# Output projection of a decoder layer: the low weights' pass of 320 token columns against two of 160

## The chip, the cores and the metric

The kernel runs on one core of one Trainium2 chip. The metric is the device time of one execution in microseconds (us). For the kernel before it is 1702.18 us, the median of 3 runs (1701.84 to 1702.85).

## The reference, cut to what matters

The program is one step of a decoder layer on 320 tokens: 256 of a prompt and 8 x 8 of samples, 2048 features wide, all in float32.

```python
xn = rms_norm(x, g_mix)
z = xn @ w_in                      # split into B, C, h, q, k, v, gate_c, gate_a
y_conv = (b_gate * conv_out) @ w_conv_out
y_attn = attn @ w_attn_out
merged = jax.nn.sigmoid(gate_c) * y_conv + jax.nn.sigmoid(gate_a) * y_attn
h = x + merged @ w_o               # the output projection: 2048 x 2048
hn = rms_norm(h, g_ffn)
h = h + (jax.nn.silu(hn @ w_gate) * (hn @ w_up)) @ w_down
```

The change lies in `merged @ w_o`.

## The kernel before, in words

Activations lie transposed: features on the 128 partitions, the `T` = 320 tokens along the free axis, one slice of 128 features per k. A product is computed as weights (128 x 128, loaded into TensorE as the stationary operand) times 320 token columns, summed over k in a PSUM tile.

To keep float32's precision with the type fp32r, every weight and every activation is split into a high part (rounded to fp32r) and a low part (the rest). A product of the two then takes three passes: high weights x high activations, high weights x low activations, low weights x high activations. Low x low is left out.

All large products go through one helper, `product` (L116 to L143). It takes two column blocks of 128 output features (`c` = 0 and 1), each with a PSUM tile `ps[c]` of its own. Weights come in tiles of four k and both column blocks (128 x 4 x 256). `load_cols` (L96) issues the transfer from SyncE's queue into `wraw` (4 buffers), ScalarE rounds it into `whi` (L93), VectorE subtracts to give `wlo` (L94; 3 buffers each). For every k and c of the tile, L133 to L137 then issue the three passes into `ps[c]`, in the order (whi, xh), (whi, xl), (wlo, xh). In the last tile of a product, all k of c = 0 come ahead of those of c = 1. A pass is one instruction of the program and two rows of the profile: the weight load (engine PEld) and the matmul (PE). Each pass loads its weights anew, also where the one before it had the same.

The order of the kernel: the k and v columns of `w_in` (a helper of their own, L284), q, then C, H, B with the convolution (L725 to L769), during which attention is interleaved as side work, then gates and the two branch outputs (L810 to L833), the output projection (L842 to L861), and the feed-forward network in two halves (L868 on).

The output projection runs over eight pairs of column blocks (`mp`) with 16 k each. Its activations are `m_h` and `m_l`, its product has the name `wo`. After each pair of blocks VectorE adds the product to the residual `hT` (L850), ScalarE and VectorE make the next high and low parts (`hh_t`, `hl_t`, L851 and L852), and GpSimd sums squares into `hacc` (L857 to L861), which the feed-forward part reads at L881, after its first gate product (`fg`). The attention's side work is not active any more in this stage.

Two other places are used as price rows below. The prompt scores (`prompt_scores`, L434) multiply queries and keys in fp32r with 256 columns (L442) and 128 columns (L447), each pass with a load of 128 weight columns. The transposes of the attention weights (`prompt_pt`, L495) move 128 columns with a load of 128 columns.

```python
for mp in range(8):                                            # L842
    c0 = mp * CW
    ps = product(
        lambda k0, n: load_cols(w_o, k0, n, c0), KC,
        lambda k: m_h[:, k, :], lambda k: m_l[:, k, :], "wo",
    )
```

Of the kernel before, what the change touches and what calls it, by code (L numbers as in the profile page):

```python
# [17 lines left out]
T = TP + NB * TS  # L18
# [8 lines left out]
P = 128  # L27
# [13 lines left out]
def hybrid_layer(ctx: ExitStack, tc: tile.TileContext, a: dict, o: list):  # L41
# [17 lines left out]
    def ps_acc(name):  # L59
        return acc.tile([P, 512], F32, tag="acc", name=name)  # L60
# [6 lines left out]
    def u(s):  # L67
        uid[0] += 1
        return f"{s}_{uid[0]}"

    def after(*marks):

        es = ExitStack()
        for m in marks:
            es.enter_context(tc.issue_after(m.ins))
        return es
# [3 lines left out]
    def tmp(tag, name):  # L80
        return wk.tile([P, UL], F32, tag=tag, name=u(name))
# [14 lines left out]
    def load_cols(w, k0, n, c0, behind=()):  # L96
        raw = raw_tile()
        nc.sync.dma_start(
            raw[:, :n, :],
            w[k0 * P:(k0 + n) * P, c0:c0 + CW].rearrange("(k p) n -> p k n", p=P),  # L100
        )
        hi, lo = part_tiles()
        with after(*behind):
            split_to(hi[:, :n, :], lo[:, :n, :], raw[:, :n, :])
        return hi, lo
# [5 lines left out]
    def tick():  # L111
        if side_work[0] is not None:
            with after(*last.values()):
                next(side_work[0], None)

    def product(load, nk, xh, xl, name, tiles=None, loaded=None, before=None, late=None):  # L116

        ps = [ps_acc(u(name)) for _ in range(2)]
        k0 = 0
        for n in tiles or [min(KT, nk - k) for k in range(0, nk, KT)]:  # L120
            hi, lo = load(k0, n)
            if loaded:
                loaded()
            order = [(k, c) for k in range(n) for c in range(2)]
            if k0 + n == nk:
                order.sort(key=lambda kc: kc[1])
            for k, c in order:
                kc = k0 + k
                if before and c == 0:
                    before(kc)  # L130
                if late and k0 + n == nk and (k, c) == (2, 1):
                    late(ps)
                for i, (w, x) in enumerate(((hi, xh), (hi, xl), (lo, xh))):  # L133
                    last["mm"] = nc.tensor.matmul(  # L134
                        ps[c][:, :T], w[:, k, c * P:(c + 1) * P], x(kc),
                        start=(kc == 0 and i == 0), stop=(kc == nk - 1 and i == 2),
                    )  # L137
            k0 += n
            while pending:
                with after(last["lo"]):  # L140
                    pending.pop(0)()
            tick()
        return ps  # L143
# [61 lines left out]
    def in_pair(c0, name, **kw):  # L205
        return product(lambda k0, n: load_cols(w_in, k0, n, c0), KC, xh, xl, name, **kw)
# [476 lines left out]
    def load_q(j, gp):  # L683
        def load(k0, n):
            raw = raw_tile()
            for two in range(2):
                c0 = O_Q + j * 512 + two * 256 + gp * P
                mark["q"] = nc.sync.dma_start(
                    raw[:, :n, two * P:(two + 1) * P],
                    w_in[k0 * P:(k0 + n) * P, c0:c0 + P].rearrange("(k p) n -> p k n", p=P),  # L690
                )
            hi, lo = part_tiles()
            for g in range(2):
                src = raw[:, :n, :].rearrange("p k (two g d) -> p k two g d", two=2, g=2)[:, :, :, g]
                dst = [
                    w[:, :n, g * P:(g + 1) * P].rearrange("p k (two d) -> p k two d", two=2) for w in (hi, lo)
                ]
                split_to(dst[0], dst[1], src)
            return hi, lo
        return load  # L700
# [17 lines left out]
    for j in range(2):  # L718
        for gp in range(2):
            ps = product(load_q(j, gp), KC, xh, xl, "q")  # L720
            pending.append(lambda j=j, gp=gp, ps=ps: q_out(j, gp, ps))
# [3 lines left out]
    for cp in range(4):  # L725
        c_sb = []
        ps = in_pair(O_C + cp * CW, "C")
# [4 lines left out]
        ps = in_pair(O_H + cp * CW, "H")  # L732
# [26 lines left out]
        ps = in_pair(O_B + cp * CW, "B")  # L759
# [18 lines left out]
    m_h = mm.tile([P, KC, T], F32R, name="m_h")  # L778
    m_l = mm.tile([P, KC, T], F32R, name="m_l")
# [15 lines left out]
    def load_ao(c0):  # L795
        def load(k0, n):
            j = k0 // KT
            raw = raw_tile()
            for par in range(2):
                r0 = (2 * j + par) * GRP * HD  # L800
                nc.sync.dma_start(
                    raw[par * 64:(par + 1) * 64, :, :],
                    w_ao[r0:r0 + GRP * HD, c0:c0 + CW].rearrange("(g d) n -> d g n", d=HD),
                )
            hi, lo = part_tiles()
            split_to(hi, lo, raw)
            return hi, lo
        return load

    for mp in range(8):  # L810
        c0 = mp * CW
        sg = {}
        for nm, off, tag in (("gc", O_GC, "ta"), ("ga", O_GA, "tb")):
            ps = in_pair(off + c0, nm)
            for c in range(2):
                t = tmp(tag, nm)[:, :T]
                nc.vector.tensor_mul(t, ps[c][:, :T], rb)
                nc.scalar.activation(t, t, AF.Sigmoid)
                sg[nm, c] = t
        ps = product(  # L820
            lambda k0, n: load_cols(w_co, k0, n, c0), 8,
            lambda k: cv_h[:, k, :], lambda k: cv_l[:, k, :], "yc",
        )
        for c in range(2):
            nc.vector.tensor_mul(sg["gc", c], ps[c][:, :T], sg["gc", c])
        ps = product(
            load_ao(c0), 8, lambda k: at_h[:, k, :], lambda k: at_l[:, k, :], "ya",
        )
        for c in range(2):
            t = sg["ga", c]  # L830
            nc.vector.tensor_mul(t, ps[c][:, :T], t)
            nc.vector.tensor_add(t, t, sg["gc", c])
            split_to(m_h[:, mp * 2 + c, :], m_l[:, mp * 2 + c, :], t)  # L833
# [8 lines left out]
    for mp in range(8):  # L842
        c0 = mp * CW
        ps = product(
            lambda k0, n: load_cols(w_o, k0, n, c0), KC,
            lambda k: m_h[:, k, :], lambda k: m_l[:, k, :], "wo",
        )
        for c in range(2):
            k = mp * 2 + c
            nc.vector.tensor_add(hT[:, k, :], ps[c][:, :T], hT[:, k, :])  # L850
            nc.scalar.activation(hh_t[:, k, :], hT[:, k, :], AF.Copy, scale=g_ffn[:, k:k + 1])  # L851
            nc.vector.scalar_tensor_tensor(  # L852
                hl_t[:, k, :], hT[:, k, :], g_ffn[:, k:k + 1], hh_t[:, k, :].bitcast(F32),
                op0=ALU.mult, op1=ALU.subtract,
            )
            if k == 0:
                nc.gpsimd.tensor_tensor(hacc, hT[:, k, :], hT[:, k, :], op=ALU.mult)  # L857
            else:
                t = tmp("tc", "sq")[:, :T]
                nc.gpsimd.tensor_tensor(t, hT[:, k, :], hT[:, k, :], op=ALU.mult)  # L860
                nc.gpsimd.tensor_tensor(hacc, hacc, t, op=ALU.add)  # L861
# [6 lines left out]
    for half in range(2):  # L868
# [67 lines left out]
# [3 lines that stand above are left out]
                lambda k0, n: load_cols(w_d, f0 + k0, n, c0), nf,  # L939
                lambda k: a_h[:, k, :], lambda k: a_l[:, k, :], "dn",  # L940
                late=next_last if half == 1 and mp == 7 else None,
            )
            if half == 1 and mp == 7:
                break
            for c in range(2):
                k = mp * 2 + c
                nc.vector.tensor_add(hT[:, k, :], hT[:, k, :], ps[c][:, :T])
            if half == 1:
                pc = [ps_aux(u("fa")) for _ in range(2)]
                for c in range(2):  # L950
                    k = mp * 2 + c
                    for t, (t0, tn) in enumerate(TOK):
                        nc.tensor.transpose(pc[c][:tn, t * P:(t + 1) * P], hT[:, k, t0:t0 + tn], ident)
                for c in range(2):
                    k = mp * 2 + c
# [7 lines left out]
    k = KC - 1  # L963
# [109 lines left out]
```

## Time and profile before

| | |
|---|---|
| median of 3 runs | 1702.18 us |
| the profiled execution | 1702.27 us |
| its span, first to last instruction | 1700.5 us |
| granted TensorE clock, mean | 0.997 |
| passes named `wo` | 768, of 128x320 |
| start of the first and the last of them | 638.8 and 751.3 us |
| length recorded for one: matmul, weight load | 310 ns, 188 ns |
| VectorE, ScalarE, GpSimd busy in 638.9 to 751.6 us | 62.0, 42.2, 29.0 us |
| DMA engines busy in that stretch | 47% |

The profile is of one execution. Its first part gives each engine's busy time, its fourth the chain of work that ended last, followed backwards from the last instruction. The chain can also be read in order of time, and the instructions of a stretch can be listed one by one (the timeline). Recorded lengths of matmuls and loads include latency, so rows of successive passes overlap; the distance between two starts tells what a pass costs in a stream. A load is listed by the tiles of the pass that it is for.

### The profile page before, as it was taken

How to read it: one execution, taken by the hardware profiler on the slowest of the kernel's cores; microseconds unless marked ns; L12 is line 12 of the kernel's file. 1: busy time of each engine (PE TensorE's matmuls, PEld its weight loads, DVE VectorE, ACT ScalarE, POOL GpSimd, SP SyncE). 2: the span in 40 equal slices, each digit the busy share in tenths (PEclk: the TensorE clock that was granted, in tenths of full speed). 3: DMA queues.
4: the chain of work that ended last, by engine and by line, in shares of the span. 5: the costliest groups of instructions: out<-in, count | busy, mean ns of one | idle time of the engine just before them, and what ended most of it. 6: DMA issues, size and time to landing. Idle time of an engine off the chain costs nothing.

```text
span 1700.5 us, 27713 instructions
## 1 busy us (share of the span) xinstructions
PE 1682.2 (99%) x11600; PEld 1670.9 (98%) x11600; DVE 863.3 (51%) x1231; ACT 643.5 (38%) x945; POOL 81.3 (5%) x127
## 2 busy tenths in 40 slices
PE   8999999999999999999999999999999999999996
PEld 7999999999999999999999999999999999999996
DVE  7667554444444445556454545433345545454443
ACT  6445443333333333334333333322233333333432
POOL 1001221000000001220000000000000000000000
PEclk9999999999999999999999999999999999999998
DMA  7754554555555544444444444444444444445442
GB/s 217 216 153 142 161 151 131 147 150 151 151 152 151 149 149 149 149 149 149 149 149 150 149 150 152 152 152 150 149 150 149 149 149 149 149 151 171 149 140 96
DMA packets 256719, 258.22 MB, mean 152 GB/s; under 512 B 9091, under 2 KB 251615, under 8 KB 256433
## 3 DMA queue, kind: packets, MB, share of 16 engines
q1 hardware_dynamic: 254128, 249.86, 47.8%
q0 software_dynamic: 2128, 5.92, 1.2%
q8 instruction: 91, 1.49, 0.4%
q10 hardware_dynamic: 336, 0.66, 0.2%
q14 instruction: 36, 0.29, 0.1%
HBM read 253.29 MB, written 5.08 MB: 152 GB/s over the span
## 4 chain that ended last, share of the span: by engine, by line
PE 95%; issue 2%; DMA 1%; DVE 1%; SPq 0%; POOL 0%; ACT 0%; DVEq 0%; POOLq 0%; ACTq 0%
PE fg L134 18%; PE fu L134 18%; PE dn L134 18%; PE wo L134 7%; PE ga L134 7%; PE gc L134 7%; PE C L134 3%; PE B L134 3%; PE H L134 3%; PE ya L134 3%; PE yc L134 3%; PE q L134 2%; DMA wraw<-in_w_in_dram 0%; DMA rel<-in_rel_bias_dram 0%; PE po L508 0%
## 5 line engine op out<-in xcount | busy, mean ns | idle before, releaser
L94 DVE TENSOR_TENSOR wlo<-wraw,whi 128x1024 fp32r<-128x1024 f32 (+1 forms) x481 | 573.8, 1195 | 703.9 <-ACT whi L93 701.3
L93 ACT ACTIVATE whi<-wraw 128x1024 fp32r<-128x1024 f32 (+1 forms) x481 | 493.3, 1030 | 852.4 <-PE dn L134 198.2
L134 PE MATMUL dn<-a_h,whi 128*128 128x320 f32 x704 | 218.5, 310 | 0.0
L134 PE MATMUL fu<-hh_t,whi 128*128 128x320 f32 x704 | 217.4, 309 | 0.0
L134 PE MATMUL dn<-a_h,wlo 128*128 128x320 f32 x704 | 217.3, 309 | 0.0
L134 PE MATMUL dn<-a_l,whi 128*128 128x320 f32 x704 | 217.2, 309 | 0.0
L134 PE MATMUL fg<-hh_t,whi 128*128 128x320 f32 x704 | 217.2, 309 | 0.0
L134 PE MATMUL fg<-hl_t,whi 128*128 128x320 f32 x704 | 217.2, 309 | 0.0
L134 PE MATMUL fg<-hh_t,wlo 128*128 128x320 f32 x704 | 217.2, 309 | 0.0
L134 PE MATMUL fu<-hl_t,whi 128*128 128x320 f32 x704 | 217.2, 308 | 0.0
L134 PE MATMUL fu<-hh_t,wlo 128*128 128x320 f32 x704 | 217.2, 308 | 0.0
L134 PEld LDWEIGHTS fu<-hl_t,whi 128*128 128x128 f32 x704 | 132.2, 188 | 0.1
L134 PEld LDWEIGHTS dn<-a_l,whi 128*128 128x128 f32 x704 | 132.2, 188 | 0.0
L134 PEld LDWEIGHTS fu<-hh_t,whi 128*128 128x128 f32 x704 | 132.2, 188 | 0.1
L134 PEld LDWEIGHTS dn<-a_h,whi 128*128 128x128 f32 x704 | 132.2, 188 | 0.0
L134 PEld LDWEIGHTS dn<-a_h,wlo 128*128 128x128 f32 x704 | 132.2, 188 | 0.0
L134 PEld LDWEIGHTS fg<-hh_t,whi 128*128 128x128 f32 x704 | 132.2, 188 | 0.0
L134 PEld LDWEIGHTS fg<-hh_t,wlo 128*128 128x128 f32 x704 | 132.2, 188 | 0.0
L134 PEld LDWEIGHTS fg<-hl_t,whi 128*128 128x128 f32 x704 | 132.2, 188 | 0.0
L134 PEld LDWEIGHTS fu<-hh_t,wlo 128*128 128x128 f32 x704 | 132.2, 188 | 0.0
L134 PE MATMUL gc<-xh_t,whi 128*128 128x320 f32 x256 | 79.6, 311 | 0.0
L134 PE MATMUL ga<-xh_t,wlo 128*128 128x320 f32 x256 | 79.4, 310 | 0.0
(285 smaller groups left out, 2934.7 us busy)
## 6 DMA issues: line engine op xcount, KB each, us to landing
wraw<-in_w_in_dram SPq DMA_DIRECT2D x119, 512.0 KB, 3.6
wraw<-in_w_gate_dram SPq DMA_DIRECT2D x88, 512.0 KB, 3.6
wraw<-in_w_up_dram SPq DMA_DIRECT2D x88, 512.0 KB, 3.6
wraw<-in_w_down_dram SPq DMA_DIRECT2D x88, 512.0 KB, 3.5
wraw<-in_w_o_dram SPq DMA_DIRECT2D x32, 512.0 KB, 3.5
wraw<-in_w_in_dram SPq DMA_DIRECT2D x34, 256.0 KB, 4.4
wraw<-in_w_conv_out_dram SPq DMA_DIRECT2D x16, 512.0 KB, 3.5
wraw<-in_w_attn_out_dram SPq DMA_DIRECT2D x32, 256.0 KB, 4.1
```

Source lines behind the costliest of these rows:

```text
L93: last["hi"] = nc.scalar.activation(hi, src, AF.Copy)
L94: last["lo"] = nc.vector.tensor_sub(lo, src, hi.bitcast(F32))
L134: last["mm"] = nc.tensor.matmul(ps[c][:, :T], w[:, k, c * P:(c + 1) * P], x(kc), start=(kc == 0 and i == 0), stop=(kc == nk - 1 and i == 2),)
```

## The change

In the output projection alone, the pass of the low weights over all 320 tokens becomes two passes, over tokens 0 to 159 and 160 to 319. They do not follow each other: the order for each k and c is (whi, m_h) over 320, (wlo, m_h) over the first 160, (whi, m_l) over 320, (wlo, m_h) over the last 160. The low weights are so loaded twice. The start flag of the accumulation stays at the first pass, the stop flag goes to the last half. All other products keep their three passes.

```diff
-    def product(load, nk, xh, xl, name, tiles=None, loaded=None, before=None, late=None):
+    def product(load, nk, xh, xl, name, tiles=None, loaded=None, before=None, late=None, uneven=False):
...
-                for i, (w, x) in enumerate(((hi, xh), (hi, xl), (lo, xh))):
+                parts = ((hi, xh, 0, T), (hi, xl, 0, T), (lo, xh, 0, T))
+                if uneven:
+
+                    h = T // 2
+                    parts = ((hi, xh, 0, T), (lo, xh, 0, h), (hi, xl, 0, T), (lo, xh, h, T))
+                for i, (w, x, t0, t1) in enumerate(parts):
                     last["mm"] = nc.tensor.matmul(
-                        ps[c][:, :T], w[:, k, c * P:(c + 1) * P], x(kc),
-                        start=(kc == 0 and i == 0), stop=(kc == nk - 1 and i == 2),
+                        ps[c][:, t0:t1], w[:, k, c * P:(c + 1) * P], x(kc)[:, t0:t1],
+                        start=(kc == 0 and i == 0), stop=(kc == nk - 1 and i == len(parts) - 1),
                     )
...
-            lambda k: m_h[:, k, :], lambda k: m_l[:, k, :], "wo",
+            lambda k: m_h[:, k, :], lambda k: m_l[:, k, :], "wo", uneven=True,
```

## The prediction

> **What bounds the kernel now.** I read first the page's part 1 (busy time of each engine), then part 4 and the chain in order of time for the stage of the change, then the output tile `wo` by itself, then the timeline of two short stretches.
>
> ```profile
> PE 1682.2 (99%) x11600; PEld 1670.9 (98%) x11600; DVE 863.3 (51%) x1231; ACT 643.5 (38%) x945; POOL 81.3 (5%) x127
> ```
>
> ```profile
> PE 95%; issue 2%; DMA 1%; DVE 1%; SPq 0%; POOL 0%; ACT 0%; DVEq 0%; POOLq 0%; ACTq 0%
> ```
>
> ```profile
> 639.00 112.65 PE wo L134 x768
> 751.65 14.08 PE fg L134 x96
> ```
>
> TensorE is the bound: 95% of the chain that ended last is PE. The third block is the chain in order of time (start, length, what): the output projection is one unbroken piece of 768 passes in 112.65 us, followed at once by the first gate product. So a pass of 320 columns costs 112.65 / 768 = 146.7 ns, which is 0.458 ns a column, and any time added to or taken from this piece moves the end by as much. Among the waits of PE there are five in the whole kernel, 1.6 us at most, and none in this stage.
>
> A pass has two parts: its 128 weight columns are loaded (row PEld), then the token columns stream (row PE). The timeline inside the stage (start, length, engine, line, operation) shows how the two overlap:
>
> ```profile
> 700.01 0.31 PE L134 MATMUL wo<-m_h,whi 128*128 128x320 f32 x1
> 700.01 0.19 PEld L134 LDWEIGHTS wo<-m_l,whi 128*128 128x128 f32 x1
> 700.15 0.31 PE L134 MATMUL wo<-m_l,whi 128*128 128x320 f32 x1
> 700.16 0.19 PEld L134 LDWEIGHTS wo<-m_h,wlo 128*128 128x128 f32 x1
> ```
>
> The load for pass i+1 starts when pass i starts, not earlier, though nothing else holds it back: one load ahead, never two. The lengths (310 and 188 ns) are latencies that overlap their neighbours; starts are what counts. While a pass streams for 146.7 ns, the load is hidden. The question of this change is what happens behind a pass of 160 columns, which streams for only 160 x 0.458 = 73.3 ns.
>
> The kernel holds a row for that: the prompt scores (L442, L447) run fp32r passes of 256, 256, 128, 128 columns, twice, between passes of 320, each with its own load of 128 columns.
>
> ```profile
> 107.17 0.28 PE L442 MATMUL ps<-k2h,at_h 128*128 128x256 f32 x1
> 107.17 0.19 PEld L442 LDWEIGHTS ps<-k2l,at_h 128*128 128x128 f32 x1
> 107.29 0.28 PE L442 MATMUL ps<-k2l,at_h 128*128 128x256 f32 x1
> 107.29 0.19 PEld L447 LDWEIGHTS ps<-k2h,at_h 128*128 128x128 f32 x1
> 107.41 0.22 PE L447 MATMUL ps<-k2h,at_h 128*128 128x128 f32 x1
> 107.41 0.19 PEld L447 LDWEIGHTS ps<-k2l,at_h 128*128 128x128 f32 x1
> 107.47 0.27 PE L447 MATMUL ps<-k2l,at_h 128*128 128x128 f32 x1
> 107.52 0.19 PEld L442 LDWEIGHTS ps<-k2h,at_h 128*128 128x128 f32 x1
> 107.58 0.33 PE L442 MATMUL ps<-k2h,at_h 128*128 128x256 f32 x1
> 107.63 0.19 PEld L442 LDWEIGHTS ps<-k2l,at_h 128*128 128x128 f32 x1
> ...
> 108.23 0.31 PE L134 MATMUL C<-xl_t,whi 128*128 128x320 f32 x1
> ```
>
> Passes of 256 follow each other at 0.12 us = 256 x 0.458. The second pass of 128 is recorded 0.06 us = 128 x 0.458 behind the first, but is 0.05 us longer than it (0.27 against 0.22), and the load after it starts only at 107.52, 0.11 us behind 107.41. The same at the next pass: 0.33 instead of 0.28, next load another 0.11 later. So the second short pass is recorded at the end of the stream before it, but then stands waiting for its weights: the load, begun at 107.41, needs about 0.11 us. A pass therefore costs the larger of its columns and one load.
>
> **The price of a load.** From the first pass of 256 (107.17) to the second of 320 (108.23) is 1060 ns, for one pass of 320, four of 256 and four of 128. Taking off 146.7 and 4 x 117.3 leaves 444.1 / 4 = 111 ns for each of the four. The eight such bursts of the trace give 110.8 to 111.5 ns. A second row: the transposes L495, 128 columns too, come six in 0.66 us in the chain, 110 ns each. Between starts of loads behind a short pass I find 107 ns at least.
>
> **The change part by part.** It touches PE alone. The order of instructions on DVE, ACT, POOL and SP is the same before and after; PE's differs only in this stage, where each pair of k and column block (16 x 2 x 8 = 256 pairs) has passes of 320, 160, 320, 160 in place of 320, 320, 320. PE has 256 instructions more.
>
> 1. Removed: 256 whole passes of the low weights, 146.7 ns each: -37.55 us.
> 2. Added: 512 half passes. Their columns alone would be 512 x 73.3 = 37.55 us, nothing net. But behind each half stands a whole pass with its own load that can begin only when the half begins, so each half takes 111 ns (the burst's row, the nearest: same type, same load, same neighbours): 512 x 111 = 56.83 us.
> 3. The whole passes are unchanged: behind each a half's load (110) hides under 146.7. Whether the half covers columns 0 to 159 or 160 to 319 changes neither count.
>
> Sum: 56.83 - 37.55 = **+19.3 us**; per pair 2 x 111 - 146.7 = 75.3 ns, x 256.
>
> Bounds. At the smallest gap of 107 ns: 2 x 107 - 146.7 = 67.3 ns, +17.2 us. At the largest wait: the pass of 320 right behind such a burst lasts up to 368 ns against the usual 309, so it stands 59 ns, after a start recorded 60 ns behind the pass before: 119 ns a half, 91.3 ns a pair, +23.4 us. A pass of 160 is in no row, but lies between those of 128 and 256, both of which go by 0.458 ns a column. A gain I exclude: columns and whole passes stay, loads only increase.
>
> What I cost at nothing. The low weights are needed one pass earlier, 0.15 us: DVE's split (L94) of this stage's tiles, matched in order, ends at least 4.39 us before the first low pass that reads it. A tile serves 8 pairs, which take 8 x 515 = 4.1 us as forecast instead of 8 x 440 = 3.52, so the splits and the transfers behind them have more room, not less; if that cover were gone, each of 32 tiles could cost up to the 0.15 us, 4.7 us. The second half reaches its PSUM columns 73 ns after the whole pass before it wrote there, instead of 147; the pairs of 128 (L447) also add to the same columns in succession, and their 111 ns already contain whatever that costs. The additions that close each product (L850 to L861) depend on the last pass as before and run beside the next product. Later stages are all PE's and can't give the time back.
>
> The trace's duration of a load row is 188 ns, its starts lie 107 to 112 ns apart. The Trainium skill, TensorE: Matmul & The Clock Gate, section LDWEIGHTS (loading the stationary operand), puts a load at its columns divided by 1.2 in ns, an estimated 107 for 128; the change would then cost about 17.1 us, the lower end that the row gives too, and the trace's bursts are slightly dearer.
>
> **The rivals.**
>
> *A: loads run ahead, no change.* If the load of the pass behind a half could start some 37 ns (110 - 73.3) before the half starts, each whole pass would lend its spare load time to the half after it: four loads of 110 ns are 440 ns, exactly the 3 x 146.7 = 440 ns that the columns take, and the time stays at 1702.3. Place: the load row of PE in this stage. Against it: in 700.01 to 700.16 the load port is free for some 37 ns of each 146.7 and the next load still waits for the pass to start; behind the whole pass of 107.29 the load for the second pass of 128 also starts only at 107.41, with the first. The Trainium skill, TensorE: Matmul & The Clock Gate, section Architectural detail: the array is 16x 32x32, not 1x 128x128, says PE's queue can pull loads ahead of passes in flight, which would be this rival if it went more than one pass deep; the trace agrees with one. Its section Back-to-back issue gap gives about 81 ns for sustained passes of 128 columns with loads, by which the estimate would be +3.9 us; this trace's 111 ns speaks against it.
>
> *B: the load is not overlapped with its predecessor.* If in this pattern a half had to wait for the full 188 ns of the load behind it: 2 x 188 - 146.7 = 229.3 ns a pair, +58.7 us, 1761. For it: the length of the load row. Against: loads begin 0.11 us apart in the burst while each is recorded at 0.19.
>
> *C: short passes lose their rate.* At four times the columns' time a half would be 293 ns, +112.6 us, 1815. Against: the passes of 128 are recorded at 222 ns, shorter than the 281 of 256.
>
> **How the numbers follow.** The profiled execution took 1702.27 us, its span 1700.5 and 1.8 around it; the median of the runs is 1702.18, 0.1 us from it. Forecast: 1702.27 + 19.3 = 1721.6. Chances: the forecast's mechanism 0.89; A 0.06; B and C 0.04 together; something that I have not seen and that gains 0.01. The range takes the bounds: 1702.27 + 17.2 = 1719.5 and 1702.27 + 23.4 = 1725.7; of the 0.89 I put 0.81 inside. Within 0.2% (3.4 us, about what a measurement of this kernel can tell from no change) is A alone, faster is the unseen 0.01, slower the rest: 0.93.
>
> **What the profile would show.** The piece `wo` in the chain goes from 112.65 us to about 132 with 1024 passes, and `fg` starts near 770.9 instead of 751.65; every later piece keeps its length. Starts of loads alternate between gaps of 0.147 and 0.111. The whole passes are recorded some 73 ns behind a half and last about 309 + 37 = 346 ns; the halves last about 237, between 222 and 281. DVE's and ACT's idle times in the stage grow by 19 us, and PE waits for nobody. If load gaps were 0.147 and 0.073 instead, A is right. I am wrong also if a wait for `wlo` appears on PE, or if the time shows up outside this stage.

## The result and the profile after

The changed kernel takes 1721.92 us, the median of 4 runs (1721.5 to 1722.5), against 1702.44 (4 runs, 1701.84 to 1702.85): a ratio of 1.0113, interval 1.0099 to 1.0126. It is 19.5 us slower. The forecast was 1721.6, 19.3 us more.

The profiled execution is the one of 1722.5 us, with a span of 1720.6. The chain in order of time (start, length, what) shows the stage and the piece behind it:

```profile
639.53 132.23 PE wo L139 x1024
771.76 14.12 PE fg L139 x96
```

112.65 us have become 132.23, so 19.58 of the 20.1 us by which this span is longer lie in this one piece. The other 0.53 us had come before it: it starts at 639.53, not 639.00, and in the runs below at 638.75 to 639.99, so this start differs from run to run. From the start of `fg` to the end of the span it is 948.8 us in both. The page's first part shows nothing of the slowdown: PE is as busy as before.

```profile
PE 1702.6 (99%) x11856; PEld 1690.8 (98%) x11856; DVE 860.8 (50%) x1231; ACT 644.6 (37%) x945; POOL 80.6 (5%) x127
```

One has to read starts. The timeline inside the stage (start, length, engine, line, operation), both rows of PE:

```profile
699.78 0.34 PE L139 MATMUL wo<-m_h,whi 128*128 128x320 f32 x1
699.82 0.19 PEld L139 LDWEIGHTS wo<-m_h,wlo 128*128 128x128 f32 x1
699.97 0.24 PE L139 MATMUL wo<-m_h,wlo 128*128 128x160 f32 x1
699.97 0.19 PEld L139 LDWEIGHTS wo<-m_l,whi 128*128 128x128 f32 x1
700.04 0.35 PE L139 MATMUL wo<-m_l,whi 128*128 128x320 f32 x1
700.08 0.19 PEld L139 LDWEIGHTS wo<-m_h,wlo 128*128 128x128 f32 x1
700.23 0.24 PE L139 MATMUL wo<-m_h,wlo 128*128 128x160 f32 x1
700.23 0.19 PEld L139 LDWEIGHTS wo<-m_h,whi 128*128 128x128 f32 x1
```

The half starts at 699.97 and with it the load for the whole pass behind it. The whole pass is recorded at 700.04, when the half's columns have gone through, but it lasts 0.35 instead of 0.31: I read this as a pass that stands waiting for that load. The next load starts at 700.08, 0.11 us behind 699.97; before, a load started within a few ns of a pass's start, so I take 700.08 for the true start of the whole pass. Over all 256 pairs the starts of loads lie 108.4 ns apart across a half and 150.0 ns across a whole pass: 2 x (108.4 + 150.0) = 516.8 ns a pair, where it was 440.

### The profile page after: what moved, and what is told of

The parts are those of the page before. It is cut to its first block, busy times and chain, and to the rows that moved or that the text cites. A ratio compares the mean times of both kernels' runs of the same rounds, so it can differ in the third digit from the quotient of the medians.

```text
span 1720.6 us, 28224 instructions
## 1 busy us (share of the span) xinstructions
PE 1702.6 (99%) x11856; PEld 1690.8 (98%) x11856; DVE 860.8 (50%) x1231; ACT 644.6 (37%) x945; POOL 80.6 (5%) x127
## 4 chain that ended last, share of the span: by engine, by line
PE 95%; issue 2%; DMA 1%; DVE 0%; ACT 0%; POOL 0%; SPq 0%; DVEq 0%; ACTq 0%; POOLq 0%
PE fg L139 18%; PE fu L139 18%; PE dn L139 18%; PE wo L139 8%; PE gc L139 7%; PE ga L139 7%; PE C L139 3%; PE B L139 3%; PE H L139 3%; PE ya L139 3%; PE yc L139 3%; PE q L139 2%; DMA wraw<-in_w_in_dram 0%; DMA rel<-in_rel_bias_dram 0%; PE po L513 0%
## 5 line engine op out<-in xcount | busy, mean ns | idle before, releaser
L139 PE MATMUL wo<-m_h,wlo 128*128 128x160 f32 x512 | 121.0, 236 | 0.0
L139 PEld LDWEIGHTS wo<-m_h,wlo 128*128 128x128 f32 x512 | 97.8, 191 | 0.0
```

The costliest lines, as they stand in the source:

```text
L139: last["mm"] = nc.tensor.matmul(ps[c][:, t0:t1], w[:, k, c * P:(c + 1) * P], x(kc)[:, t0:t1], start=(kc == 0 and i == 0), stop=(kc == nk - ...
```

## The experiments

**Theory L**, that of the forecast: one load runs ahead, so a pass costs the larger of its columns (0.458 ns each) and the load for the pass behind it (about 108 ns by the trace of the changed kernel), and a whole pass that had to wait costs 150.0 instead of 146.7. **Rival R**: a pass more costs a fixed 76.5 ns a pair, whatever its columns; it fits the result as well. Others stand with the run that they belong to. Only the list of passes for the output projection is edited, as `(weights, activations, first token, end)`; the run with narrow loads adds a width in weight columns.

### Order alone: e1_order_only

```diff
-                    parts = ((hi, xh, 0, T), (lo, xh, 0, h), (hi, xl, 0, T), (lo, xh, h, T))
+                    parts = ((hi, xh, 0, T), (lo, xh, 0, T), (hi, xl, 0, T))
```

> One part of the change alone: the order (whi, m_h), (wlo, m_h), (whi, m_l), with all three passes whole. Theory L (a pass costs the larger of its columns and one weight load, and only one load runs ahead): every load of about 108 ns hides under 146.7 ns, so the stage takes 112.65 us and the whole 1702.3 us, no change. Rival R (each pass more costs a fixed 76.5 ns per pair, whatever its columns): no pass more, no change either. Rival O (the changed order itself, which swaps the weights at every pass and needs the low weights earlier, is part of the 19.6 us): up to some us over 1702.3.

Measured: 1702.34 us against 1702.45 (ratio 0.9999, 0.9990 to 1.0008), and in the chain:

```profile
639.00 112.65 PE wo L137 x768
```

The piece is as long as before, to 0.01 us. Rival O falls: the order, the swap of weights at every pass and the earlier use of the low weights cost nothing. All of the 19.6 us is the split.

### Split without alternation: e2_adjacent

```diff
+                    parts = ((hi, xh, 0, T), (hi, xl, 0, T), (lo, xh, 0, T // 2), (lo, xh, T // 2, T))
```

> The split without the alternation: whole, whole, half, half. Theory L: two halves at one load each, 108.4 ns, and one whole pass behind a stall at 150.0 instead of two: 146.7 + 150.0 + 2 x 108.4 = 513.5 ns a pair, stage 131.5 us, whole 1721.2 us; the alternation buys nothing. Rival R: one pass more, 516.7 ns, stage 132.3 us, 1722. Rival A' (a whole pass between the halves shelters a part of their loads): dearer than the changed kernel, over 1722.5.

Measured: 1722.79 us (1722.44 to 1723.43) against 1702.45, ratio 1.0117 (1.0100 to 1.0134); the stage took 133.07 us, 519.8 ns a pair:

```profile
638.75 133.07 PE wo L137 x1024
```

None of the three had it: for the stage L was 1.6 us too low, R 0.8. Rival A' has the sign, by 0.8 us of stage. Starts of loads lie 108.7 and 111.8 ns apart across the first and the second half, 151.0 and 148.6 across the whole passes; no half is sheltered, and both here and in the changed kernel each costs about one load. The alternation is worth 133.07 - 132.23 = 0.84 us of the 20, one trace each.

### Unequal parts: e3_224_96 and e4_288_32

```diff
+                    parts = ((hi, xh, 0, T), (lo, xh, 0, 224), (hi, xl, 0, T), (lo, xh, 224, T))
```

> Low pass split into 224 and 96 columns, alternating as in the changed kernel. Columns alone would be 102.7 and 44 ns, both under one load, so theory L: both cost one load, pair 2 x (108.4 + 150.0) = 516.8 ns, stage 132.3 us, whole 1721.9 us, as with 160 and 160. Rival R: the same. A theory by which the part of the load that a short pass leaves uncovered grows with how short it is, and is not made good by the other, gives the same sum too; one by which only passes under some number of columns are slow would differ from 160 and 160 by some us.

Measured: 1721.05 us against 1702.45 (1.0107, 1.0091 to 1.0122); stage 131.36 us, 513.1 ns a pair, 0.9 us less than forecast. The chain, and the starts of the loads in the timeline:

```profile
638.82 131.36 PE wo L137 x1024
```

```profile
699.90 0.19 PEld L137 LDWEIGHTS wo<-m_l,whi 128*128 128x128 f32 x1
...
700.01 0.19 PEld L137 LDWEIGHTS wo<-m_h,wlo 128*128 128x128 f32 x1
...
700.16 0.19 PEld L137 LDWEIGHTS wo<-m_h,whi 128*128 128x128 f32 x1
...
700.27 0.19 PEld L137 LDWEIGHTS wo<-m_h,wlo 128*128 128x128 f32 x1
```

Passes of 224 columns (699.90 to 700.01) and of 96 (700.16 to 700.27), 102.7 and 44 ns by their columns, both cost 108.4 ns from load to load. The 96 columns are less than half of the 224, at the same price. The 0.9 us lie in a whole pass: behind the 224 columns it takes 150.0 ns, as in the changed kernel, but behind the 96 only 146.7; why is not shown.

```diff
+                    parts = ((hi, xh, 0, T), (lo, xh, 0, 288), (hi, xl, 0, T), (lo, xh, 288, T))
```

> Low pass split into 288 and 32 columns, alternating. 288 columns take 132.0 ns, more than a load, so theory L: 132.0 + 108.4 for the two, and one whole pass at 150.0 and one at 146.7: 537.1 ns a pair, stage 137.5 us, whole 1727.1 us: dearer than 160 and 160 by 5.2 us. Rival R (a fixed price for each pass more): 132.3 us, 1721.9 us.

Measured: 1726.41 us against 1702.45 (1.0137, 1.0122 to 1.0152), and in the chain and the timeline:

```profile
638.89 137.01 PE wo L137 x1024
```

```profile
699.94 0.29 PE L137 MATMUL wo<-m_h,wlo 128*128 128x288 f32 x1
...
700.07 0.19 PEld L137 LDWEIGHTS wo<-m_h,wlo 128*128 128x128 f32 x1
...
700.22 0.18 PE L137 MATMUL wo<-m_h,wlo 128*128 128x32 f32 x1
700.22 0.19 PEld L137 LDWEIGHTS wo<-m_h,whi 128*128 128x128 f32 x1
700.24 0.39 PE L137 MATMUL wo<-m_h,whi 128*128 128x320 f32 x1
700.33 0.19 PEld L137 LDWEIGHTS wo<-m_h,wlo 128*128 128x128 f32 x1
```

The 288 columns exceed a load and are paid in full, 131 ns (699.94 to 700.07); the 32 columns still cost a load, 700.22 to 700.33. L had said 137.5 us for the stage. R had said 132.3 and falls here: the price does not hang on the number of passes alone. Columns moved from a pass that is shorter than a load to one that is longer have to be paid for.

### A stream of halves: e5_halves_all_k

```diff
+                    parts = (*(((hi, xh, 0, T),) if kc == 0 else ((hi, xh, 0, 160), (hi, xh, 160, T))), (hi, xl, 0, 160), (hi, xl, 160, T), (lo, xh, 0, 160), (lo, xh, 160, T))
```

> Every pass of the output projection in halves, six passes of 160 columns for each k and column block (the first pass at k = 0 stays whole), so that the stage is a stream of short passes: the price of a load by itself. Theory L: 240 pairs x 6 x 108.4 ns + 16 pairs x (150.0 + 4 x 108.4) = 165.4 us, whole 1755 us, gaps between starts of loads 108 throughout. Rival R (76.5 ns for each pass more): 170.2 us, 1760 us. Rival A (loads run ahead when the queue lets them) can't hide them here either.

Measured: 1760.12 us against 1702.53 (1.0338, 1.0322 to 1.0353); stage:

```profile
639.10 170.26 PE wo L137 x1520
```

Here R's number is right and L's is 5 us too low. In the stream loads start 111.6 ns apart, not 108.4. So the 3.3 ns that I had ascribed to a whole pass behind a wait are paid at nearly every load that holds up its pass, whichever row of the trace they show up in. In two halves in succession it is the same: the first half, which had its weights in time, costs 108.7 ns, the second, which had to wait for them, 111.8; and in the bursts of the kernel before, the gaps are 107 to 109 ns across the first short pass of two and 110 to 113 across the second. With 111.7 ns for a short pass and 146.7 for every whole pass, L gives 240 x 6 x 111.7 + 16 x (146.7 + 4 x 111.7) = 170.3 us. R's 76.5 is the same sum in other words (2 x 111.7 - 146.7 = 76.7) and can't be told apart from it where all parts are halves.

### Narrower loads: e6_narrow_loads

```diff
+                    parts = ((hi, xh, 0, T), (lo, xh, 0, 160, 64), (lo, xh, 160, T, 64), (hi, xl, 0, T))
...
+                        ps[c][:m1, t0:t1], w[:, k, c * P:c * P + m1], x(kc)[:, t0:t1],
```

> Whole, half, half, whole, with the halves' loads of 64 weight columns instead of 128; the low weights' part of the other 64 output features of each block is left out. Theory L: behind the first half stands a load of 64 columns, about 54 ns, hidden under 73.3; behind the second the load of 128 for a whole pass: 146.7 + 73.3 + 108.4 + 150.0 = 478.4 ns a pair, stage 122.5 us, whole 1712 us. Rival M (any short pass has a least length of about 108 ns, whatever is loaded behind it): 513.5 ns, 131.5 us, 1721 us, as with two halves in succession and full loads.

Measured: 1712.08 us against 1702.53 (1.0057, 1.0041 to 1.0074); the stage, the rows of the tile `wo` (least, median and largest length in ns), and the loads in the timeline:

```profile
639.20 122.31 PE wo L138 x1024
```

```profile
L138 PEld LDWEIGHTS wo<-m_h,wlo x512: 133/134/135, 639.0 to 761.0; 128*64 128x64 f32 x171
L138 PE MATMUL wo<-m_h,wlo x512: 234/236/238, 639.2 to 761.1; 128*64 128x160 f32 x171
L138 PEld LDWEIGHTS wo<-m_h,whi x256: 188/191/192, 638.9 to 760.7; 128*128 128x128 f32 x128
```

```profile
699.94 0.19 PEld L138 LDWEIGHTS wo<-m_l,whi 128*128 128x128 f32 x1
...
700.05 0.19 PEld L138 LDWEIGHTS wo<-m_h,whi 128*128 128x128 f32 x1
...
700.20 0.28 PEld L138 LDWEIGHTS wo<-m_h,wlo 128*64 128x64 f32 x2
...
700.41 0.19 PEld L138 LDWEIGHTS wo<-m_l,whi 128*128 128x128 f32 x1
```

A load of 64 columns is recorded at 134 ns, one of 128 at 188: 54 ns for 64 columns. By that, as an estimate, about 107 of the 188 are the 128 columns, and the rest is latency that overlaps. With the narrow load behind it the first half costs 73.6 ns, its columns: 700.20 to 700.41 is one whole pass (145.9) and this half. The second half, with the same narrow load of its own but one of 128 behind it, costs 108.3 (699.94 to 700.05). As many passes as in the changed kernel, 10 us less: rival M, a least length of the pass itself, falls, and so does R again; L had 122.5 us for the stage. It is the load that sets the price, and the load of the pass *behind*.

### Half of the low pass left out: e7_left_out

```diff
+                    parts = ((hi, xh, 0, T), (lo, xh, 0, T // 2), (hi, xl, 0, T))
```

> The low weights' second half pass is left out (tokens 160 to 319 lack it): 320, 160, 320. Theory L: the half still costs one load and leaves the next whole pass a restart: 146.7 + 108.4 + 150.0 = 405.1 ns a pair, stage 103.7 us, whole 1693.4 us: half of a pass's columns go, 18.8 us, and 9 us are saved. By columns alone: 366.7 ns, 93.9 us, 1683.5 us.

Measured: 1694.16 us against 1702.53 (0.9950, 0.9936 to 0.9965); stage 104.11 us, 406.7 ns a pair, where L had 103.7 us and the columns alone 93.9:

```profile
639.99 104.11 PE wo L137 x768
```

Dropping 18.8 us of columns saves 8.5: 160 columns cost about three quarters of 320.

### Together

With 111.7 ns for a short pass that a full load holds up, a value chosen after the runs, and 146.7 for every whole pass, the sums for a pair are 516.8 (changed kernel; 516.5 measured), 516.8 (two halves in succession; 519.8), 516.8 (224 and 96; 513.1), 537.1 (288 and 32; 535.2), 478.4 (narrow loads; 477.8) and 405.1 (left out; 406.7) ns. None is off by more than 3.7 ns, under 1 us of a stage. What decides between 146.7 and 150 ns for a whole pass, and so makes up this rest, stays open.

## Why the prediction was right, point by point

- *What bounds the kernel*: held. The piece `wo` carried the loss one for one, no wait of PE appeared in the stage, and the stages behind it took 948.8 us as before.
- *Step 1 and the columns of step 2*: held. A half's columns take 73 ns (the next pass is recorded 72.5 to 73.7 ns behind it); a pass of 160, in no row before, goes by 0.458 ns a column as those of 128 and 256 did.
- *Step 2, 111 ns for a half*: held as a sum. Measured (132.23 - 512 x 0.1467) / 512 = 111.6 ns. The second row, the transposes, was weaker than it looked: their loads of 128 columns are recorded at 140 ns, not 188, so their 110 ns a pass need not be the price of such a load.
- *Step 3, whole passes unchanged*: not quite. From load to load a half takes 108.4 ns, not 111, and 3.3 more show in the whole pass behind it, 150.0 instead of 146.7. The burst's 111 was taken over the whole burst, passes behind a wait included (right behind a short one, those of 256 columns take 119 to 121 ns, not 117), so it had both in it and the sum was right: 19.3 forecast, 19.58 measured in the stage. Taking the two apart by the changed kernel's trace then misled the expectation for the stream of halves by 5 us.
- *Costed at nothing*: held. The order and the earlier low weights cost 0.00 us (order alone). That run has no halves and so says nothing of the PSUM columns that the second half reaches sooner; the changed kernel's trace does: starts of loads lie 108.3 ns apart across the first half and 108.5 across the second.
- *Signs in the profile*: 1024 passes and about 132 us were right; whole passes last 346 and 348 ns (346 forecast), halves 236 (237); gaps between loads were 0.150 and 0.108 where 0.147 and 0.111 had been said. VectorE's and ScalarE's idle time in the stage grew by 21 and 19 us (19 forecast). `fg` starts at 771.76, not 770.9: 0.53 of it lies ahead of the stage.
- *Rival A*: refused by the result (516.5 ns a pair, not 440) and by the timeline: behind a half, no load starts before the half does. Alternating gave 0.84 us. *B* (1761 us) and *C* (1815, by a factor of four that no row here shows) are far off.
- The price by the Trainium skill, TensorE: Matmul & The Clock Gate, section LDWEIGHTS (loading the stationary operand), an estimated 107 ns for 128 columns, agrees with the 54 ns for 64 of the narrow loads; the stream of halves pays 111.6, and the measurement decides. The about 81 ns for a pass of 128 columns with its load, in the Trainium skill, TensorE: Matmul & The Clock Gate, section Back-to-back issue gap, do not hold for the fp32r passes of 128 columns in the bursts, which cost 111.

## What to carry to other kernels

In a stream of passes with a load each, a pass costs the larger of its own columns and the load for the pass behind it; here, for a load of 128, the two meet at an estimated 111 / 0.458 = 240 columns, and the runs have that point between 224, which still cost a load, and 288, which cost their columns. By the same sum a split costs nothing only while both parts stay above that, which no run here tried. Long neighbours lend a short pass next to nothing (0.84 us of 20), since one load at most runs ahead. Price a new shape from a burst in the same trace that has the same neighbours, start to start, and take the burst's whole sum: the recorded lengths (188 for a load that costs 108) and single gaps mislead, and the busy share of PE stays at 99% throughout.

## What the runs showed of the hardware that was not expected

- Behind a pass of 32 columns the next is recorded 27 ns later, where 32 x 0.458 would be 14.7; 96 and 224 columns come close to the rule (44.1 and 101.0 ns, against 44.0 and 102.6). The Trainium skill, TensorE: Matmul & The Clock Gate, section Wait — 56ns, not 53.3ns?, gives a floor of about 25 ns between starts; the recorded starts agree. It cost nothing here, under a load of 108.
- A load that holds up the pass behind it costs 108.3 to 109.0 ns when the pass that it runs under had its own weights in time, and 111.6 to 111.8 when that one had waited too. Why a wait adds some 3 ns to the pass that waited, and did not for the whole pass behind 96 columns (146.7), is not shown.
